# A two-layer hybrid attention trunk on one core: keys transposed and copied in four pieces, rotary roots in two, partial sums of the first squares, a new order for the first output chunk

## The chip, the cores and the metric

The kernel runs on one core of a Trainium2 chip. The metric is the device time of one execution, in microseconds (us). Three timed runs of the kernel before gave 1242.74, 1245.52 and 1246.12 us; the median is 1245.52. A core has a matrix engine (TensorE, in the profile PE, its weight loads PEld), a vector engine (VectorE, DVE), a scalar engine (ScalarE, ACT), a further vector engine (GpSimd, POOL) and an engine that here issues the transfers (SyncE, SP). Each engine runs its own instructions in the order in which the program lists them, and waits where an operand or a buffer is not ready.

## The reference

Two groups of tokens, a prompt of 512 and a sample of 256, with 1024 channels, go through two layers with the same weights. In each layer:

```
mod = silu(c) @ w_ada + b_ada ; shift, scale, gate = split(mod, 3)
hid = rms_norm(x, norm_g) * (1 + scale) + shift
qa, ka, va, za, qb, kb, vb, zb, ga, gb = split(hid @ w_in)
oa = neighbourhood attention(qa, ka, va, rpb)      # 8 heads of 64, 8 x 16 window
ya = (oa * silu(za)) @ w_pa
qh = rope(rms_norm(qb)) ; kh = rope(rms_norm(kb))  # per head, 8 query heads, 2 key heads
ob = softmax(qh kh^T / 8) vb                       # 4 query heads share a key head
yb = (ob * silu(zb)) @ w_pb
x  = x + gate * ((sigmoid(ga) * ya + sigmoid(gb) * yb) @ w_out)
```

After the second layer a last `rms_norm` gives the two outputs. All of it is float32.

## The kernel before, in words

**Precision.** TensorE gets each float32 operand as a rounded high part and a low part, and a product is three matmuls: high·high, high·low, low·high. So each weight half (128x1024) that arrives in a `raw` tile is first copied to its high part by ACT (`whi`, L222), and DVE (for a few halves POOL) subtracts to get the low part (`wlo`, L228). `split_one` issues the pair. `ahead` calls it at chosen steps of the chunk before, and `low_all` issues the waiting subtraction two steps later. Every operand that attention makes is split in the same way, with a copy on ACT and a subtraction on DVE.

**Steps.** The long stretches are built of steps (`step`): the matmuls of two 128-channel pieces of the contraction for 128 output rows, 6 matmuls of 128x512 for the prompt or 12 of 128x256 (four pieces) for the sample. After each step the program issues what is due: work put off by `defer(k, fn)` until k steps later, one piece of a `chain` (the normalisation of the next layer), attention pieces from `slots` at a set rate, and side sums of the next layer's modulation. No engine reorders anything, so the place where a piece is issued sets when it can run and what waits behind it.

**A layer.** First the values of the neighbourhood attention (`va`), then four chunks of query and key pairs with eight attention heads in slots, each head 8 slots after the one before. A head's slots 0 to 16 (`na_slots`) hold: scores, bias and row maximum, exponentials (L775) and their normalisation in slots 0 to 5; three transposes of the probabilities (`trans(0)` in slot 6, `trans(1)` in 7, `trans(2)` in 10), each copied by ACT one slot later (`ev`, L699) and completed by DVE (`el`, L704) one slot after that; the product with the values for the prompt (`pv_p`, tile `op`, slot 10) and for the sample (`pv_s`, tile `os`, slot 14). `op` and `os` share one PSUM buffer. Each is emptied by ACT (`o1`, tile `otmp`, L689) and then by DVE (`o2`, tile `oa`, L694), in slots 11 and 12 for `op` and 15 and 16 for `os`.

Then come the queries `qb` and keys and values `kvb` of the second attention with norm and rotation. `rope_part` sums squares and rotates, `rope_finish` takes the inverse square roots with three Newton rounds on DVE (L358 to L365, after L1326) and scales the rotated rows (L1333). TensorE transposes them (`qt`, `kt` by L1418) through two PSUM buffers (`ps_t`) and ACT and DVE split them into `GQ` and `GK` (L667, L668, L675, L676, L679, L680). The offsets of these pieces, in steps, stand in the table `SC`: QF, QT, QS, QST for the queries, KF for `rope_finish` of the keys, KT for their transpose, SGQ for the first slot of the grouped attention. Around them run the gate chunks `za`, whose PSUM results pass ACT (`zt`, `zh`), DVE (L1440, `zl` L1454) and POOL (L1443). The grouped attention runs in slots (`gsp` scores, maximum L902, exponential L912).

At the end of a layer the merged rows go through the output projection, four chunks for the prompt (`wo`, `feat_chunk` with `groups=(0,)`, two row blocks m of four steps each), then the sample. `merged` is split on DVE at L1563. After DP steps (last layer: DPE) the chain of the next normalisation starts: sum of squares `a_`, Newton rounds `b_` on DVE, a broadcast of the roots by matmul `c_` (tile `rb`), then one piece per channel block.

**The start.** Loads of x, of the first modulation weights (`adaraw`) and of the first weight halves are issued by SP at planned times (`load`, T0 us after the start, U us per unit). A small planner (`run_jobs`) sorts jobs of known length by earliest start, `lag` us after what they depend on. The squares of the eight 128-channel blocks of x (ACT) are added into one tile, six additions on DVE and one on POOL, and `sq_sum` sums it over partitions with four matmuls into `ssps`. WARM puts 18 matmuls of zeros (`junk`, 128x512) ahead of all, and one more every 0.45 us of planned time until 18 us.

## Time and profile before

| view | what it gives |
|---|---|
| timed runs | 1242.74, 1245.52, 1246.12 us, median 1245.52 |
| profiled execution | 1244.36 us, span from first to last instruction 1242.6 us |
| PE busy | 1208.7 us, 97% of the span, 7282 instructions |
| DVE busy | 818.4 us, 66% |
| ACT busy | 580.6 us, 47% |
| POOL busy | 347.6 us, 28% |
| mean granted TensorE clock | 0.995 |
| chain that ended last | PE 78%, DVE 11%, ACT 5% |

A row of the timeline gives start, length, engine, line, operation, output tile <- input tiles, shape and count; in brackets stands how long the engine had been idle just before, and the engine, tile and line that ended it. A row of the waits gives the engine that waited, for what, the total in us, the number of waits and the longest. A row of the windows gives the stretch, its length and, engine by engine in the order PE, PEld, DVE, ACT, POOL, the busy us with the count of instructions, then the granted TensorE clock of that stretch (PEclk, 1 is full speed), the DMA share and its GB/s.

### The profile page before, as it was taken

The page shows a single profiled execution, that of the slowest core. Times are in us where ns is not written, and L with a number is a line of the kernel's source. Part 1 is how long each engine was busy: PE and PEld are TensorE (multiplying, and loading weights), DVE is VectorE, ACT ScalarE, POOL GpSimd, SP SyncE. Part 2 cuts the span into 40 slices and gives each one's busy share as a digit, 9 for nine tenths or more (in the row PEclk, how much of TensorE's full clock was granted, in tenths as well). Part 3 has the DMA queues.
Part 4 walks back from the last instruction along what each step waited for, and adds up shares of the span by engine and source line. Part 5 has one row for each costly group of instructions (what it writes and reads, how often), then busy time and mean ns, then how long its engine had stood idle before and what let it go on. Part 6 is the DMA issues. An engine that isn't in the chain of part 4 may idle for free.

```text
span 1242.6 us, 19501 instructions
## 1 busy us (share of the span) xinstructions
PE 1208.7 (97%) x7282; PEld 1058.6 (85%) x7282; DVE 818.4 (66%) x1609; ACT 580.6 (47%) x1229; POOL 347.6 (28%) x383
## 2 busy tenths in 40 slices
PE   8999999989999999999989999998999999999997
PEld 5789988879898988887888998897988998888887
DVE  5757877775556558998384688777566545683435
ACT  4447755445545332333153776554555543232323
POOL 0024555342223121121131443553322212121102
PEclk9999999999999999999999999999999999999999
DMA  9343411111011234556352324112011113332334
GB/s 350 138 124 94 108 54 54 49 51 35 26 44 51 69 107 149 170 169 202 119 172 88 93 74 124 35 38 65 18 52 52 35 35 102 119 105 66 119 102 152
DMA packets 48125, 118.28 MB, mean 95 GB/s; under 512 B 5408, under 2 KB 11936, under 8 KB 48032
## 3 DMA queue, kind: packets, MB, share of 16 engines
q1 hardware_dynamic: 47888, 116.98, 30.6%
q8 instruction: 57, 0.93, 0.3%
q14 instruction: 36, 0.29, 0.1%
q10 hardware_dynamic: 144, 0.07, 0.0%
HBM read 110.74 MB, written 6.29 MB: 94 GB/s over the span
## 4 chain that ended last, share of the span: by engine, by line
PE 78%; DVE 11%; ACT 5%; issue 3%; DMA 1%; POOL 1%; SPq 0%; DVEq 0%; ACTq 0%; POOLq 0%
PE accp L115 35%; PE accs L115 17%; PE accw L115 8%; PE go L115 3%; PE gsp L115 3%; PE gtp L937 3%; PE acct L115 3%; DVE adaacc L445 3%; DVE wlo L228 2%; ACT p L775 1%; PE sp L115 1%; PE op L115 1%; ACT whi L222 1%; PE adap L115 1%; DVE ptl L704 1%
## 5 line engine op out<-in xcount | busy, mean ns | idle before, releaser
L115 PE MATMUL accp<-hh,whi 128*128 128x512 f32 x512 | 204.3, 399 | 0.0
L115 PE MATMUL accp<-hh,wlo 128*128 128x512 f32 x512 | 201.2, 393 | 2.1 <-DVE wlo L228 2.1
L115 PE MATMUL accp<-hl,whi 128*128 128x512 f32 x512 | 201.2, 393 | 0.0
L228 DVE TENSOR_TENSOR wlo<-raw,whi 128x1024 fp32r<-128x1024 f32 x119 | 159.1, 1338 | 21.1 <-ACT whi L222 20.5
L115 PE MATMUL accs<-hh,whi 128*128 128x256 f32 x512 | 146.4, 286 | 0.0
L115 PE MATMUL accs<-hh,wlo 128*128 128x256 f32 x512 | 145.0, 283 | 0.0
L115 PE MATMUL accs<-hl,whi 128*128 128x256 f32 x512 | 144.9, 283 | 0.0
L926 POOL TENSOR_TENSOR gp<-gp,gss 128x512 f32<-128x512 f32 x80 | 83.4, 1042 | 213.8 <-DVE gss L924 192.5
L222 ACT ACTIVATE whi<-raw 128x1024 fp32r<-128x1024 f32 x124 | 129.7, 1053 | 17.7 <-PE accw L115 8.2
L115 PEld LDWEIGHTS accp<-hh,wlo 128*128 128x128 f32 x512 | 96.8, 189 | 24.9 <-DVE wlo L228 3.8
L115 PEld LDWEIGHTS accp<-hl,whi 128*128 128x128 f32 x512 | 97.1, 190 | 17.5
L115 PEld LDWEIGHTS accp<-hh,whi 128*128 128x128 f32 x512 | 96.8, 189 | 17.7
L699 ACT ACTIVATE pth<-gtp 128x512 fp32r<-128x512 f32 x80 | 47.7, 597 | 111.2 <-PE go L115 90.2
L115 PEld LDWEIGHTS accs<-hh,whi 128*128 128x128 f32 x512 | 98.2, 192 | 1.0
L115 PEld LDWEIGHTS accs<-hl,whi 128*128 128x128 f32 x512 | 98.2, 192 | 1.0
L115 PEld LDWEIGHTS accs<-hh,wlo 128*128 128x128 f32 x512 | 98.0, 191 | 0.0
L1539 POOL TENSOR_TENSOR th<-th 128x512 f32<-128x512 f32 (+1 forms) x32 | 43.5, 1371 | 171.2 <-DVE th L1532 171.2
L445 DVE SCALAR_TENSOR_TENSOR adaacc<-adaraw,csil,adaacc 128x512 f32<-128x512 f32 x112 | 86.6, 829 | 3.6 <-DMA adaraw<-in_wsd 3.6
L722 POOL TENSOR_TENSOR bm<-u,masks 128x128 f32<-128x128 f32 (+2 forms) x80 | 41.3, 539 | 152.4 <-DMA u<-in_rpb 152.4
L704 DVE TENSOR_TENSOR ptl<-gtp,pth 128x512 fp32r<-128x512 f32 x80 | 54.7, 685 | 40.5 <-ACT pth L699 40.4
L115 PE MATMUL accw<-whi,hh 128*128 128x512 f32 x192 | 77.3, 403 | 0.0
L115 PE MATMUL accw<-wlo,hh 128*128 128x512 f32 x192 | 75.3, 392 | 0.0
(245 smaller groups left out, 2965.7 us busy)
## 6 DMA issues: line engine op xcount, KB each, us to landing
raw<-in_wst SPq DMA_DIRECT2D x124, 512.0 KB, 3.6
adaraw<-in_wsd SPq DMA_DIRECT2D x64, 256.0 KB, 3.1
adaraw<-in_wad SPq DMA_DIRECT2D x32, 256.0 KB, 6.0
u<-in_rpb SPq DMA_DIRECT2D x16, 354.5 KB, 4.8
u<-in_rpb SPq DMA_DIRECT2D x16, 236.5 KB, 4.4
out_y<-y SPq DMA_DIRECT2D x12, 256.0 KB, 2.5
x<-in_xT SPq DMA_DIRECT2D x8, 256.0 KB, 5.0
res<-in_xT SPq DMA_DIRECT2D x8, 256.0 KB, 3.0
```

The costliest lines, as they stand in the source:

```text
L115: T.matmul(out=out, lhsT=lhsT, rhs=rhs, start=start, stop=stop, skip_group_check=True)
L222: A.activation(out=hi, in_=r, func=AF.Copy)
L228: eng.tensor_sub(out=lo, in0=r, in1=hi.bitcast(F32))
L445: V.scalar_tensor_tensor(out=acc[n, h, g], in0=r, scalar=c, in1=acc[n, h, g], op0=ALU.mult, op1=ALU.add)
L699: A.activation(out=h, in_=t, func=AF.Copy)
L704: V.tensor_sub(out=lo, in0=t, in1=h.bitcast(F32))
L722: G.tensor_tensor(out=o.rearrange("p (c r) -> p c r", r=r), in0=u, in1=mk.rearrange("p (c r) -> p c r", r=r), op=ALU.add)
L775: A.activation(out=P[:, j, :], in_=P[:, j, :], func=AF.Exp, scale=-1.0, bias=ss[:, j:j + 1], accum_out=ss[:, 2 + j:3 + j])
L926: G.tensor_mul(out=pv_, in0=pv_, in1=ss[:, 4:4 + n].unsqueeze(2).to_broadcast([128, n, w]))
L937: T.transpose(t[:, q, 128 * j:128 * j + 128], src, ident)
L1539: G.tensor_add(out=t[:, sl], in0=t[:, sl], in1=mrg[k][:, sl])
```

## The change

Seven places are changed; what is computed stays the same except for the order of the sum of the first squares.

- **Start.** 16 `junk` matmuls ahead, and further ones only where the planner has a gap on PE until 20 us: 25 in place of 46. T0 goes from 3.6 to 4.3 and `lag` from 0.12 to 0.22. Of the eight squares, blocks 1 to 3 are added into 0 on DVE, 5 into 4 on POOL, and `sq_sum` runs on the four tiles 0, 4, 6 and 7.
- **Neighbourhood attention.** `pv_p`, its `o1` and its `o2` go one slot later (11, 12, 13); `trans(2)`, `ev(2)` and `el(2)` stay, and so does the sample's part.
- **Rotary part.** `newton` can be called in parts. `rope_finish` does the first half of the roots at once, the second half one step later, and the scaling of the i-th tile 2 + i steps later. QF 5 to 4, QT 9 to 10, QS 6 to 5, QST 12 to 11.
- **Keys.** KF 7 to 5, KT 13 to 9, SGQ 16 to 13. The transpose of the prompt's keys is issued at KT, that of the sample's two steps later, and in each the copy of the second key head follows one step after the first.
- **Weights.** For chunks whose contraction has four pieces (`pa`, `pb`), `ahead` is called after steps 2 and 4, not 3 and 6.
- **First output chunk.** `late=True`: the last step of both row blocks comes after all others.
- **Next layer's norm.** An empty piece between `b_` and `c_`, and DP 6 to 5: in the first layer's prompt `a_` and `b_` come one step earlier and `c_` where it was; for the sample and at the end of the last layer, `c_` comes one step later.

```diff
 SC = dict(
-    T0=3.6,
+    T0=4.3,
-    WARM=(18, 18.0, 0.45),
+    WARM=(16, 20.0),
-    QF=5,
-    QT=9,
+    QF=4,
+    QT=10,
-    QS=6,
-    QST=12,
-    KF=7,
-    KT=13,
-    SGQ=16,
+    QS=5,
+    QST=11,
+    KF=5,
+    KT=9,
+    SGQ=13,
-    DP=6,
+    DP=5,
...
     def paired(pieces):
-        return pieces[0:3] + [sum(pieces[i:i + 2], []) for i in range(3, len(pieces), 2)]
+        return pieces[0:4] + [sum(pieces[i:i + 2], []) for i in range(4, len(pieces), 2)]
...
-        return [[a_], [b_], [c_]]
+        return [[a_], [b_], [], [c_]]
...
+            kk = per * (1 + g)
+            seq = [(m, k0) for m in range(2) for k0 in range(0, nk, kk)]
+            if late:
+                seq = [p for p in seq if p[1] < nk - kk] + [p for p in seq if p[1] == nk - kk]
+            for m, k0 in seq:
...
-                        if not (keep and name[2] == 3) and cnt[0] in ((3, 6) if len(groups) == 2 else (3, 5) if groups[0] == 0 else (2, 3)):
+                        if not (keep and name[2] == 3) and cnt[0] in ((2, 4) if nk == 4 else (3, 6) if len(groups) == 2 else (3, 5) if groups[0] == 0 else (2, 3)):
                             ahead(name)
...
-        at(10, pv_p)
         at(10, lambda: trans(2))
-        at(11, lambda: o1(NP))
+        at(11, pv_p)
         at(11, lambda: ev(2))
-        at(12, lambda: o2(0, NP))
+        at(12, lambda: o1(NP))
         at(12, lambda: el(2))
+        at(13, lambda: o2(0, NP))
         at(14, pv_s)
...
-        def run_jobs(lag=0.12):
+        def run_jobs(lag=0.22):
...
+            n0, until = SC["WARM"]
+            t = 2.0 + 0.35 * n0
+            for j in sorted((j for j in jobs if j["eng"] == "PE"), key=lambda j: done[j["n"]]):
+                start = done[j["n"]] - j["dur"]
+                while t + 0.5 < min(start, until):
+                    out.append((t, -1, lambda: warm(1)))
+                    t += 0.3
+                t = max(t, done[j["n"]])
+            warm(n0)
...
-        jg = job("POOL", 1.2, [js[2], js[3]], lambda: sq_add(0, 3, 2, G), 1)
-        j = js[0]
-        for k, d in ((1, js[1]), (4, js[4]), (2, jg), (5, js[5]), (6, js[6]), (7, js[7])):
-            j = job("DVE", 0.75, [j, d], lambda k=k: sq_add(0, k, 0, V), 1)
-        j = job("PE", 0.95, [j], sq_sum, 0)
+        ja = js[0]
+        for k in range(1, 4):
+            ja = job("DVE", 0.85, [ja, js[k]], lambda k=k: sq_add(0, k, 0, V), 1)
+        jb = job("POOL", 1.3, [js[4], js[5]], lambda: sq_add(0, 5, 4, G), 1)
+        jsum = []
+        for k, d in ((0, ja), (4, jb), (6, js[6]), (7, js[7])):
+            jsum.append(job("PE", 0.95, [d] + jsum[-1:], lambda k=k: sq_sum(k, k == 0, k == 7), 0))
...
             def rope_finish(rs, ss):
...
-                y = newton(ss.rearrange("p t h -> p (t h)"), n * nh).rearrange("p (t h) -> p t h", h=nh)
+                y, parts = newton_parts(ss.rearrange("p t h -> p (t h)"), n * nh)
...
+                roots()
+                defer(1, roots2)
...
+                    defer(2 + i, lambda r=r, k=k, t=t: V.tensor_mul(
+                        out=r, in0=r, in1=yv[:, t:t + k, :].unsqueeze(3).to_broadcast([128, k, nh, 64])))
...
+            def ktr(g):
+                c, n = RNG[g]
...
+                evac_k(GK[0][0], GK[0][1], 0, t, slice(c, c + n))
+                defer(1, lambda: evac_k(GK[1][0], GK[1][1], 1, t, slice(c, c + n)))
...
             defer(SC["KF"], kfin)
-            defer(SC["KT"], ktr)
+            defer(SC["KT"], lambda: ktr(0))
+            defer(SC["KT"] + 2, lambda: ktr(1))
...
                 feat_chunk(("wo", l, i), merged, KC, lambda m, g, ps, i=i: wev(m, g, ps, i), groups=(0,),
-                           keep=i >= 2)
+                           keep=i >= 2, late=i == 0)
```

**PE at the start.** `adap` are the first modulation products (four matmuls of one pair of loads), `adat` their columns, `ssps` the sum of squares, `rb` the broadcast of its roots. Before:

```order
L115 MATMUL junk<-cst 128x512 x29
L115 MATMUL adap<-adaraw,c_104 32x256 x4
L115 MATMUL junk<-cst 128x512 x3
L115 MATMUL adap<-adaraw,c_104 32x256 x4
L115 MATMUL junk<-cst 128x512 x2
L115 MATMUL ssps<-ones,sq 128x1 x4
L115 MATMUL junk<-cst 128x512 x2
L115 MATMUL adat<-sel,rows 128x2 x2
L115 MATMUL junk<-cst 128x512
L115 MATMUL adap<-adaraw,c_104 32x256 x4
L115 MATMUL junk<-cst 128x512
```

After the change:

```order
L115 MATMUL junk<-cst 128x512 x22
L115 MATMUL ssps<-ones,sq 128x1 x8
L115 MATMUL adap<-adaraw,c_104 32x256 x4
L115 MATMUL ssps<-ones,sq 128x1 x4
L115 MATMUL adap<-adaraw,c_104 32x256 x8
L115 MATMUL ssps<-ones,sq 128x1 x4
L115 MATMUL adat<-sel,rows 128x2 x2
L115 MATMUL adap<-adaraw,c_104 32x256 x4
L115 MATMUL junk<-cst 128x512 x3
L115 MATMUL adap<-adaraw,c_104 32x256 x4
L115 MATMUL rb<-ident,ny 128x128 x4
```

The one group of four `ssps` becomes four groups, two of them ahead of the first product, one behind it and one behind the third. The junk between the products is gone but for three, and `rb`, which came after four products, comes after five.

**ACT around the end of the second neighbourhood head**, first layer. `p,ss` are exponentials of the next head, `pth` the high part of a transpose, `Q` query copies of a chunk. Before:

```order
L667 ACTIVATE Q<-accp 64x128
L667 ACTIVATE Q<-accp 64x384
L689 ACTIVATE otmp<-op 64x512
L699 ACTIVATE pth<-tp 128x512
L775 ACTIVATE p,ss<-p,ss 128x256 x2
L222 ACTIVATE whi<-raw 128x1024
L667 ACTIVATE Q<-accp 64x128
L667 ACTIVATE Q<-accp 64x384
L775 ACTIVATE p,ss<-p,ss 128x256 x2
L689 ACTIVATE otmp<-os 64x256
```

After the change:

```order
L680 ACTIVATE Q<-accp 64x128
L680 ACTIVATE Q<-accp 64x384
L712 ACTIVATE pth<-tp 128x512
L788 ACTIVATE p,ss<-p,ss 128x256 x2
L222 ACTIVATE whi<-raw 128x1024
L680 ACTIVATE Q<-accp 64x128
L680 ACTIVATE Q<-accp 64x384
L702 ACTIVATE otmp<-op 64x512
L788 ACTIVATE p,ss<-p,ss 128x256 x2
L702 ACTIVATE otmp<-os 64x256
```

The copy of `op` (`otmp<-op`, 64x512) moved behind a transpose, two exponentials, a weight half and two query copies; the copy of `os`, which needs the same PSUM buffer, stays where it was and has two instructions between.

**The key stage on PE**, first layer. `accs` and `accp` are the sample's and the prompt's rows of the gate chunk, `kt` the transposes of the keys. Before:

```order
L115 MATMUL accs<-hh_699,whi 128x256
L115 MATMUL accs<-hl_700,whi 128x256
L115 MATMUL accs<-hh_699,wlo 128x256
L115 MATMUL accp<-hh_343,whi 128x512
L115 MATMUL accp<-hl_344,whi 128x512
L115 MATMUL accp<-hh_343,wlo 128x512
L115 MATMUL accp<-hh_356,whi 128x512
L115 MATMUL accp<-hl_357,whi 128x512
L115 MATMUL accp<-hh_356,wlo 128x512
L1418 MATMUL kt<-ident,rr 128x128 x6
L115 MATMUL accp<-hh_415,whi 128x512
```

After the change:

```order
L115 MATMUL accs<-hh_655,whi 128x256
L115 MATMUL accs<-hl_656,whi 128x256
L115 MATMUL accs<-hh_655,wlo 128x256
L1446 MATMUL kt<-ident,rr 128x128 x4
L115 MATMUL accs<-hh_674,whi 128x256
L115 MATMUL accs<-hl_675,whi 128x256
L115 MATMUL accs<-hh_674,wlo 128x256
```

The key transposes stood behind the 48 `accs` of the first gate chunk and the first 6 `accp` of the next one; now the prompt's four stand behind 12 of these `accs`, three sample steps and one prompt step earlier, and the sample's two come two steps after them.

**DVE in the same stage.** `rr` are the scaled keys that `kt` reads, `zl` and `zt` the gate chunk, `GK` the low parts of the keys. Before:

```order
L1333 TENSOR_TENSOR rr<-rr,ny 128x512
L1333 TENSOR_TENSOR rr<-rr,ny 128x256
L1454 TENSOR_TENSOR zl<-zt,zh 128x512
L1440 SCALAR_TENSOR_TENSOR zt<-zt,accp 128x512
L1454 TENSOR_TENSOR zl<-zt,zh 128x512
L679 TENSOR_TENSOR GK<-kt,GK 64x512
L680 TENSOR_TENSOR GK<-kt,GK 64x512
L679 TENSOR_TENSOR GK<-kt,GK 64x512
L680 TENSOR_TENSOR GK<-kt,GK 64x512
L679 TENSOR_TENSOR GK<-kt,GK 64x256
```

After the change:

```order
L1470 SCALAR_TENSOR_TENSOR zt<-zt,accp 128x512
L228 TENSOR_TENSOR wlo<-raw,whi 128x1024
L1365 TENSOR_TENSOR rr<-rr,ny 128x512
L1365 TENSOR_TENSOR rr<-rr,ny 128x256
L1484 TENSOR_TENSOR zl<-zt,zh 128x512
L692 TENSOR_TENSOR GK<-kt,GK 64x512
L693 TENSOR_TENSOR GK<-kt,GK 64x512
L1470 SCALAR_TENSOR_TENSOR zt<-zt,accp 128x512
L692 TENSOR_TENSOR GK<-kt,GK 64x512
L693 TENSOR_TENSOR GK<-kt,GK 64x512
L692 TENSOR_TENSOR GK<-kt,GK 64x256
L693 TENSOR_TENSOR GK<-kt,GK 64x256
```

The low parts of the second key head follow a gate piece, and ahead of the scaling of the keys stand a gate piece and a weight half that stood ahead of the roots before.

More of the change, by code (lines that the diff above doesn't have):

```diff
@@ L365, in newton @@
             V.scalar_tensor_tensor(out=y, in0=a, scalar=1.5, in1=y, op0=ALU.add, op1=ALU.mult)
+        return y, [first, refine, refine, refine]
+    def newton(x, n):
+        y, parts = newton_parts(x, n)
+        for fn in parts:
+            fn()
         return y
@@ L563, in wide_pass, with feat_chunk @@
         wts.pop(name)
-    def feat_chunk(name, src, nk, evac, ksteps=2, groups=(0, 1), keep=False, sep=False):
+    def feat_chunk(name, src, nk, evac, ksteps=2, groups=(0, 1), keep=False, sep=False, late=False):
         cur = {}
@@ L583, in feat_chunk @@
         for g in groups:
-            for m in range(2):
-                kk = per * (1 + g)
-                for k0 in range(0, nk, kk):
+            kk = per * (1 + g)
[3 more added lines that the diff above has]
+            for m, k0 in seq:
                     def f(g=g, m=m, k0=k0, kk=kk):
@@ L1149, in sq_add, with sq_sum @@
             gfree(sq.pop((g, k)))
-        def sq_sum():
-            hcell["ps"] = ps_acc.tile([128, 4], F32, tag="acc", name="ssps")
+        def sq_sum(k, first, last):
+            if first:
+                hcell["ps"] = ps_acc.tile([128, 4], F32, tag="acc", name="ssps")
             for i in range(4):
-                mm(hcell["ps"][:, i:i + 1], sq[0, 0][:, 128 * i:128 * i + 128], ones[:, 0:1], i == 0, i == 3)
-            gfree(sq.pop((0, 0)))
+                mm(hcell["ps"][:, i:i + 1], sq[0, k][:, 128 * i:128 * i + 128], ones[:, 0:1],
+                   first and i == 0, last and i == 3)
+            gfree(sq.pop((0, k)))
         js = [job("ACT", 0.63, [], lambda k=k: square(0, k), 1, tx[k]) for k in range(KC)]
-        jg = job("POOL", 1.2, [js[2], js[3]], lambda: sq_add(0, 3, 2, G), 1)
-        j = js[0]
-        for k, d in ((1, js[1]), (4, js[4]), (2, jg), (5, js[5]), (6, js[6]), (7, js[7])):
-            j = job("DVE", 0.75, [j, d], lambda k=k: sq_add(0, k, 0, V), 1)
-        j = job("PE", 0.95, [j], sq_sum, 0)
-        jsum = [j]
-        for (fn,), (eng, dur) in zip(rms_chain(0, hcell)[1:], (("DVE", 2.4), ("PE", 1.0))):
+        ja = js[0]
[5 more added lines that the diff above has]
+            jsum.append(job("PE", 0.95, [d] + jsum[-1:], lambda k=k: sq_sum(k, k == 0, k == 7), 0))
+        j = jsum[-1]
+        for (fn,), (eng, dur) in zip([p for p in rms_chain(0, hcell)[1:] if p], (("DVE", 2.4), ("PE", 1.0))):
             j = job(eng, dur, [j], fn, 0)
@@ L1195, in sample_sum @@
             sums[0][0]()
-        sums = rms_chain(1, scell)
+        sums = [p for p in rms_chain(1, scell) if p]
         j = job("PE", 0.4, jadd + [jfin[0, 3], jfin[1, 3], jva[-6]], sample_sum, 0)
```

53 lines of the change are left out of this document (23 added, 30 removed).

## The prediction

> **What bounds the kernel now.** First the page's busy time, then the waits of PE.
>
> ```profile
> span 1242.6 us, 19501 instructions
> PE 1208.7 (97%) x7282; PEld 1058.6 (85%) x7282; DVE 818.4 (66%) x1609; ACT 580.6 (47%) x1229; POOL 347.6 (28%) x383
> ```
>
> ```profile
> PE gsp L115 <- ACT gp L912: 5.6, 2, 3.6
> PE op L115 <- DVE ptl L704: 5.2, 4, 1.6
> PE gsp L115 <- DVE GK L680: 4.1, 2, 2.0
> PE rb L115 <- DVE ny L365: 3.1, 2, 1.7
> PE accp L115 <- DVE wlo L228: 2.7, 5, 1.0
> PE adap L115 <- DMA adaraw<-in_wad: 1.4, 1, 1.4
> ```
>
> PE is the bound: 97% busy, and its matmuls stay the same but for some junk. So the change can only win PE's stops. These six rows hold 22.1 us, and each has an edit that touches it. A stop costs some 0.15 us beyond its idle time, since the matmul that restarts lasts longer (0.39 against 0.28 in the first row below). The second thing to win is the clock, which falls behind two of the stops:
>
> ```profile
> 165.80 0.39 PE L115 MATMUL op<-ptl,v 128*128 128x256 f32 x1 [1.00 <-DVE ptl L704]
> 201.12 0.39 PE L115 MATMUL op<-ptl,v 128*128 128x256 f32 x1 [1.61 <-DVE ptl L704]
> 247.94 0.50 PE L115 MATMUL gsp<-GK,GQ 128*128 128x512 f32 x1 [2.03 <-DVE GK L680]
> 256.60 0.80 PE L115 MATMUL gsp<-GK,GQ 128*128 128x512 f32 x2 [3.60 <-ACT gp L912]
> 854.25 0.64 PE L115 MATMUL gsp<-GK,GQ 128*128 128x512 f32 x1 [2.03 <-DVE GK L680]
> 862.92 0.73 PE L115 MATMUL gsp<-GK,GQ 128*128 128x512 f32 x2 [2.04 <-ACT gp L912]
> ```
>
> ```profile
> 248.00:250.00 2.00, 2.00 (x9) 1.66 (x10) 1.96 (x4) 0.00 (x0) 0.00 (x0) 1.00 0.00 0
> 258.00:260.00 2.00, 2.00 (x7) 1.55 (x6) 1.16 (x5) 1.22 (x3) 1.20 (x2) 0.50 0.44 74
> 856.00:858.00 2.00, 2.00 (x7) 1.58 (x5) 1.93 (x6) 0.00 (x0) 0.10 (x1) 0.53 0.00 0
> ```
>
> In these windows (the eighth figure is the granted clock) seven matmuls start in 2 us at half clock, nine at full clock: behind 256.60 and 854.25 six or seven 128x512 matmuls stand 0.43 us apart in place of 0.23, with the slower ones around them about 1.7 us in each layer. The 2.03 us stop at 247.94 left the clock at 1.00, the equal one at 854.25 did not.
>
> **Keys and rotary part.** The four rows from 201.12 on show what goes: in the first layer 1.76 + 2.18 + 3.75 + 1.7 (clock) = 9.4, in the second the same 1.76 (its stop is one of the four in the second row of the waits), 2.18 + 2.19 + 1.7, so 7.8; together 17.2. What comes in their place? Each edit asks DVE for the keys earlier:
>
> ```profile
> 212.00:240.00 28.00, 28.00 (x191) 25.84 (x190) 24.92 (x57) 13.04 (x28) 11.39 (x14) 1.00 0.21 64
> 233.59 0.28 PE L115 MATMUL accs<-hh,whi 128*128 128x256 f32 x1
> 240.74 0.82 PE L1418 MATMUL kt<-ident,rr 128*128 128x128 f32 x6
> 223.86 1.39 DVE L668 SCALAR_TENSOR_TENSOR GQ<-qt,GQ 64x512 fp32r<-64x512 f32 x2
> 234.44 1.26 DVE L1326 TENSOR_SCALAR qss<-qss 128x12 f32<-128x12 f32 x1
> 233.47 2.21 POOL L1443 TENSOR_TENSOR zt<-zt,oa 128x512 f32<-128x512 f32 x1 [0.18 <-DVE zt L1440]
> 238.08 1.03 DVE L1333 TENSOR_TENSOR rr<-rr,ny 128x512 f32<-128x512 f32 x2
> ```
>
> The first `kt` moves from 240.74 to 12 `accs` matmuls (0.12 each, 1.44) after 233.59: PE wants it at 235.0. It reads `rr`, and DVE's list ahead of `rr` is as long as before: it runs at 238.08, or 1.1 earlier if the small L1326 doesn't again last 1.26 while POOL works on the gate (the second part, 0.17, follows that end). With half of the 1.03 for the first tile, `rr` is there at 237.5, so PE stops 2.5 us. The bounds: nothing, if DVE uses up its 28 − 24.92 = 3.1 idle us in this stretch; 2.5 + 1.8 = 4.3, if PE brings along the 1.76 won at 201.12 and DVE doesn't. I take 2.8, as DVE is 89% busy. The queries add a second stop: two steps fewer lie between the prompt's last `qt` and the sample's first, and that needs a PSUM buffer which DVE empties with L668 late in this same list; between 0 and one such pair and its copy, 2.8; I take 1.2. With 0.15 this makes 4.1 a layer, 8.2 in both, and I count one clock drop (1.7) for two stops of 2.8, which lie between the 2.03 that dropped it once of two times and the 3.60 that did. Behind `kt`, the scores come 5.7 us later (three steps of 1.44 and one of 1.37), while the copies of one head need 2 x 0.59 and 2 x 0.69, so the old stop at 247.94 doesn't return; the one at 256.60 was DVE and ACT being late from the eight copies in a row, and these are now spread. Sum: 17.2 − 8.2 − 1.7 = **+7.3**.
>
> On the clock the Trainium skill says something else ("TensorE: Matmul & The Clock Gate", section on what is actually happening): the gate closes after an idle window of about 3.4 us, so a 2.8 us stop would cost no clock and the sum would be 9.0. The trace disagrees in one row, where 2.03 us were enough; I keep the 1.7.
>
> **Neighbourhood heads.** `pv_p` one slot later gives `ptl` a step (1.4 us) more: the stop at 165.80 and its like in the second layer go, 2 x 1.15 = +2.3. But `op` and `os` share a PSUM buffer, and `os` stays:
>
> ```profile
> 114.34 0.59 ACT L689 ACTIVATE otmp<-op 64x512 f32<-64x512 f32 x1
> 116.44 1.05 ACT L222 ACTIVATE whi<-raw 128x1024 fp32r<-128x1024 f32 x1
> 117.51 0.65 ACT L667 ACTIVATE Q<-accp 64x128 fp32r<-64x128 f32 x2
> 115.97 0.69 DVE L694 SCALAR_TENSOR_TENSOR oa<-op,otmp 64x512 f32<-64x512 f32 x1
> 118.20 0.28 PE L115 MATMUL os<-pth,v 128*128 128x256 f32 x1
> ```
>
> In the second head the copy of `op` now stands behind the second pair of Q. Without it that pair ends 0.6 earlier, at 117.55; the copy ends at 118.15 and `oa` (0.69) near 118.9, while PE wants `os` at 118.20: a new wait of 0.75. It holds the whole PE queue, since all later steps stand behind. Over two layers −1.5; the bounds are 0 (the rest of ACT's list has room) and −2.5 (the next heads, with less than 1 us left, wait too). Net **+0.8**.
>
> **Weights, the output chunk and the next norm.**
>
> ```profile
> 482.02 0.50 PE L115 MATMUL accp<-hh,wlo 128*128 128x512 f32 x1 [0.25 <-DVE wlo L228]
> 1087.58 0.50 PE L115 MATMUL accp<-hh,wlo 128*128 128x512 f32 x1 [1.04 <-DVE wlo L228]
> 568.84 0.50 PE L115 MATMUL accp<-ml,whi 128*128 128x512 f32 x1 [1.32 <-DVE ml L1563]
> 623.90 1.16 PE L115 MATMUL rb<-ident,ny 128*128 128x128 f32 x8 [1.42 <-DVE ny L365]
> 648.33 0.71 PE L115 MATMUL rb<-ident,ny 128*128 128x128 f32 x4 [1.69 <-DVE ny L365]
> 619.75 1.63 DVE L358 TENSOR_SCALAR ny<-ms 128x4 int32<-128x4 int32 x1
> 618.86 2.49 POOL L228 TENSOR_TENSOR wlo<-raw,whi 128x1024 fp32r<-128x1024 f32 x1 [1.09 <-ACT whi L222]
> ```
>
> The five `wlo` stops, 2.7 us and 5 x 0.15 (two of them are shown), are each shorter than the step or two by which `ahead` moves, so all go: **+3.4**; if ACT's or DVE's queue is the late one they stay (0). The last step of the first output block behind seven others gives `ml` far more than 1.32: **+1.5**. The first `rb` keeps its step while its roots start one step of 1.4 us earlier, but L358 (1.63 in place of 0.17) ends only with POOL's `wlo`, whose place doesn't move: of 1.57 I count +0.5 (0 to 1.57). The second gets a step of its own, +1.5 of 1.84. Together **+2.0**.
>
> **The start.**
>
> ```profile
> 11.04 1.22 PE L115 MATMUL adap<-adaraw,c 128*32 128x256 f32 x8 [1.43 <-DMA adaraw<-in_wad]
> 10.00:12.00 2.00, 0.96 (x8) 0.32 (x8) 1.69 (x4) 0.83 (x2) 0.00 (x0) 1.00 1.05 396
> 24.84 0.50 PE L115 MATMUL accw<-whi,hh 128*128 128x512 f32 x1
> 24.00:40.00 16.00, 16.00 (x133) 10.65 (x126) 10.37 (x21) 7.70 (x16) 0.00 (x0) 1.00 1.04 392
> ```
>
> From 24 to 40 us PE and the transfers (share 1.04) are both full, so only what happens ahead of 24.84 can win, and the loads pace that: junk taken away mostly leaves PE waiting for the same loads. The first roots still wait for the last square. The bounds are −2 (the last partial sum stands behind a product that waits for its load, by as much as the 1.43 of the stop at 11.04 and a product) and +2 (1.43 and one product won); I take **+0.6**, a single product of about 0.6 (half of the 1.22 for a pair).
>
> **Sum.** 7.3 + 0.8 + 3.4 + 1.5 + 2.0 + 0.6 = 15.6. The profiled execution took 1244.36, so 1228.8; the runs' median of 1245.52 is 1.2 above it, so about 1229.5 as a median.
>
> **Rivals.**
> - *Clean key stage.* DVE uses its 3.1 idle us and neither `kt` nor `qt` stops, so the 8.2 and the clock's 1.7 come on top: 1219.5. For it speaks that ACT is busy for only 13.04 of the 28 us; against it DVE's 24.92.
> - *DVE holds the key stage.* `kt` 4.3, `qt` 2.8 and a clock drop in both layers: 17.2 − 2 x (7.4 + 1.7) = −1.0 in place of 7.3, total 7.3: 1238.
> - *Nothing.* The same, and the `rb` and start terms at their lower ends: 7.3 − 2.0 − 2.6 = 2.7: 1243.
> - *Slower: the clock at the start.* 21 of the 46 junk matmuls are gone, and between 7 and 24 us PE has only short groups between waits. If the clock stays at half, the 16.0 us of PE work in the window from 24 to 40 last twice as long, +16, and the products and `rb` before them add about 4: +20 − 15.6 = 4.4, about 1250. It decides if the granted clock is still near 0.5 at 24.84. For it: 2.03 us of idleness halved it at 854.25. Against it: the 1.43 stop at 11.04 left it at 1.00, the 16 + 6 junk ahead remain, and 1.7 us of dense work opened it again each time. The Trainium skill's page named above, section on HAM oscillation, warns of gaps over 3.4 us; with that few such gaps fit here.
>
> **How the numbers follow.** Main forecast 0.53, clean stage 0.18, DVE-held stage 0.17, nothing 0.07, slower 0.05. Main's own range goes from 1224 (`kt` and `qt` at half, +4.1, no `os` wait, +1.5) to 1234 (a second clock drop, −1.7, `os` at its bound, −1.0, `rb` at nothing, −2.0). For 8 in 10 I go to 1219 and 1239. About 0.3% (3.7 us) is what a measurement can tell from no change: the first three cases are beyond it, so faster 0.88, same 0.07, slower 0.05.
>
> **What would show it.** Right: no `gsp` row with an idle time over 1 us in the key stage, a `kt` row with 2 to 4 us behind `rr`, an `os` row in the second head with some 0.75 behind `oa`, no `wlo` or `ml` rows among PE's waits. Wrong: a `kt` row without wait, the old `gsp` stops still there, a window before 40 us with a clock under 0.9, or new stops at scores because the softmax is behind.

## The result

The changed kernel takes 1256.62 us (median of 4 runs, 1253.5 to 1257.46) against 1245.33 for the kernel before (4 runs): a ratio of 1.009, 95% interval 1.0067 to 1.0112. It is slower by 11 us, where 16 us of gain were forecast. PE is busy for 1213.7 us, 5.0 more than before, and the span grew by 12.2 us to 1254.8.

The waits of PE in the changed kernel (what waited, for what; total us, times, longest):

```profile
PE sp L115 <- DVE ss L781: 7.5, 6, 1.7
PE kt L1446 <- DVE rr L1365: 5.8, 2, 2.9
PE os L115 <- DVE oa L707: 3.8, 4, 1.6
PE qt L1406 <- DVE GQ L681: 3.3, 2, 1.7
PE ssps L115 <- POOL sq L1171: 2.3, 1, 2.3
PE rb L115 <- DVE ny L369: 1.9, 2, 1.6
PE accs L115 <- POOL wlo L228: 1.8, 2, 1.6
PE gsp L115 <- ACT gp L925: 1.6, 2, 1.3
```

Nearly every row at which the edits aimed is gone or shorter: no `op`, no `accp <- wlo`, no `ml`, no `gsp <- GK`; `rb` keeps one stop of 1.64 us. In their place stand others. The timeline of PE shows them in order, from the start to the end of the first layer:

```profile
12.40 1.05 PE L115 MATMUL ssps<-ones,sq 128*128 128x1 f32 x8 [2.27 <-POOL sq L1171]
118.68 0.36 PE L115 MATMUL sp<-Kh,Q 128*128 128x256 f32 x1 [1.66 <-DVE ss L781]
126.05 0.39 PE L115 MATMUL os<-pth,v 128*128 128x256 f32 x1 [1.59 <-DVE oa L707]
176.78 0.38 PE L115 MATMUL sp<-Kh,Q 128*128 128x256 f32 x1 [1.59 <-DVE ss L781]
232.99 0.30 PE L1406 MATMUL qt<-ident,rr 128*128 128x128 f32 x1 [1.67 <-DVE GQ L681]
249.92 1.09 PE L1446 MATMUL kt<-ident,rr 128*128 128x128 f32 x4 [2.90 <-DVE rr L1365]
638.16 0.39 PE L115 MATMUL accs<-mh,wlo 128*128 128x256 f32 x1 [1.60 <-POOL wlo L228]
656.00 0.71 PE L115 MATMUL rb<-ident,ny 128*128 128x128 f32 x4 [1.64 <-DVE ny L369]
```

Behind the first of these stops the granted clock (the eighth figure) is at half for ten us:

```profile
14.00:24.00 10.00, 10.00 (x60) 6.34 (x57) 3.34 (x15) 1.82 (x3) 0.00 (x0) 0.51 1.02 369
```

Where the time went is seen when the same matmul is looked up in both timelines (start in us):

| matmul | before | changed | later by | so the stage ahead of it |
|---|---|---|---|---|
| first `accw` | 24.84 | 28.89 | 4.05 | start +4.1 |
| first `accw` of the queries | 154.69 | 164.16 | 9.47 | heads, first layer, +5.4 |
| a gate chunk behind the grouped attention | 420.09 | 429.75 | 9.66 | queries and keys +0.2 |
| an `accp` of the last `pa`/`pb` chunks | 552.17 | 559.92 | 7.75 | weights −1.9 |
| first pair chunk, second layer | 672.03 | 678.32 | 6.29 | output, norm −1.5 |
| its `accw` of the queries | 760.84 | 772.68 | 11.84 | heads +5.6 |
| behind its grouped attention | 1024.85 | 1037.84 | 12.99 | queries and keys +1.2 |
| last output chunk | 1206.66 | 1218.67 | 12.01 | weights −1.0 |

The last heads still run beside the queries. Counted to the last `os` of each layer (209.22 and 815.53 before, 217.92 and 826.43 changed) the heads cost 4.7 and 4.6 us, and the queries and keys behind them 1.0 and 2.1.

### The profile page after: what moved, and what is told of

Its sections match the earlier page's. It is cut to its first block, busy times and chain, and to the rows that moved or that the text cites. A ratio compares the mean times of both kernels' runs of the same rounds, so it can differ in the third digit from the quotient of the medians.

```text
span 1254.8 us, 19456 instructions
## 1 busy us (share of the span) xinstructions
PE 1213.7 (97%) x7285; PEld 1060.8 (85%) x7285; DVE 814.5 (65%) x1606; ACT 580.0 (46%) x1229; POOL 348.8 (28%) x383
## 3 DMA queue, kind: packets, MB, share of 16 engines
HBM read 110.74 MB, written 6.29 MB: 93 GB/s over the span
## 4 chain that ended last, share of the span: by engine, by line
PE 79%; DVE 10%; ACT 5%; issue 2%; DMA 2%; POOL 1%; SPq 0%; DVEq 0%; ACTq 0%; POOLq 0%
PE accp L115 36%; PE accs L115 17%; PE accw L115 9%; PE go L115 3%; PE gsp L115 3%; PE gtp L950 3%; PE acct L115 2%; DVE wlo L228 2%; ACT p L788 1%; PE sp L115 1%; DMA raw<-in_wst 1%; DVE GQ L681 1%; PE adat L115 1%; PE op L115 1%; DVE ptl L717 1%
```

## The experiments

In each, the kernel before ran on the same chip, and ratios are against it.

**The parts alone.** Four kernels, each the one before with one part of the diff.

```diff
-    T0=3.6,
+    T0=4.3,
-    WARM=(18, 18.0, 0.45),
+    WARM=(16, 20.0),
...
+            jsum.append(job("PE", 0.95, [d] + jsum[-1:], lambda k=k: sq_sum(k, k == 0, k == 7), 0))
```

> The kernel before with the start part alone (16 junk matmuls ahead and gaps only, planner's lag and T0, the four partial sums). Theory: with the junk gone PE stops about 2 us for POOL's sum of the squares, the clock halves from about 14 to 24 us, and the first accw comes about 4 us later than the 24.84 of before: +4 us in all. Rival: the 2.27 us stop was the chance of late loads in one execution, and the start is worth what was predicted, -0.6 us (between -2 and +1). A granted clock near 0.5 between 14 and 24 us speaks for the theory, 1.00 for the rival.

1247.38 against 1243.53 us, ratio 1.0029 (1.0014 to 1.0044): +3.9 us, spread from 1243.3 to 1250.9. The profiled execution was the fastest, had no such wait and a clock of 1.00; the mean clock of the seven others lay at 0.989 to 0.991, where it is 0.995 before. So the start costs in most executions and not by one late load, and their lower mean clock points to the clock; no profile of this kernel shows such an execution.

```diff
-        at(10, pv_p)
         at(10, lambda: trans(2))
-        at(11, lambda: o1(NP))
+        at(11, pv_p)
         at(11, lambda: ev(2))
-        at(12, lambda: o2(0, NP))
+        at(12, lambda: o1(NP))
         at(12, lambda: el(2))
+        at(13, lambda: o2(0, NP))
```

> The kernel before with the neighbourhood part alone (product with the values, its copy and its sum one slot later). Theory: the new stops at sp and os that the changed kernel shows come from this part, +4 to +5 us a layer, +8 to +10 us in all, with the two stops at op (1.0 us) gone. Rival, as predicted: the op stops go (-2.3), os waits 0.75 us a layer, -0.8 us in all; the sp stops then come from another part. The rows of sp with an idle time decide.

1259.45 us, ratio 1.0130 (1.0117 to 1.0143): +16 us, more than the whole change. The six `sp` stops (7.5 us) and the `os` stops are all here, so they come from this part. ACT's timeline of this kernel points to a cause:

```profile
100.31 0.50 ACT L786 ACTIVATE p<-p,ss 128x256 f32<-128x256 f32 x1
103.01 0.60 ACT L710 ACTIVATE pth<-tp 128x512 fp32r<-128x512 f32 x1 [2.11 <-PE op L115]
104.61 0.60 ACT L700 ACTIVATE otmp<-op 64x512 f32<-64x512 f32 x1
```

The copy `pth` of the third transposes waits 2.11 us for PE's `op`, from which it reads nothing. `pth` comes from a pool of two buffers (`ptp`), and both hold the transposes that `op` is still to read. Before, `op` was issued a slot ahead of this copy; now it is issued in the same slot, so ACT stands until PE has come to `op` and finished it, and everything behind it in ACT's and then DVE's queue is late.

```diff
-    QST=12,
-    KF=7,
-    KT=13,
-    SGQ=16,
+    QST=11,
+    KF=5,
+    KT=9,
+    SGQ=13,
...
+                defer(1, roots2)
...
-            defer(SC["KT"], ktr)
+            defer(SC["KT"], lambda: ktr(0))
+            defer(SC["KT"] + 2, lambda: ktr(1))
```

> The kernel before with the rotary and key part alone (roots in two, keys in four pieces, new offsets). Prediction on record: -7.3 us, kt waits about 2.8 us a layer and the old stops at gsp go. Reading of the changed kernel: qt waits 2 us, kt 2.9 us, a clock drop in one layer, and the scores afterwards return less than was thought: between 0 and +4 us in all.

1242.93 us, ratio 0.9994 (0.9986 to 1.0003): no difference that can be told. The old stops at `op` (1.61 us) and for `GK` are gone, the one for `gp` is down to 1.31 us in each layer, and these rows stand in the first layer (the second is alike):

```profile
223.31 0.30 PE L1396 MATMUL qt<-ident,rr 128*128 128x128 f32 x1 [1.69 <-DVE GQ L679]
223.94 0.85 PE L1396 MATMUL qt<-ident,rr 128*128 128x128 f32 x3 [0.34 <-DVE rr L1355]
240.47 0.63 PE L1436 MATMUL kt<-ident,rr 128*128 128x128 f32 x4 [1.57 <-DVE rr L1355]
253.30 0.73 PE L115 MATMUL gsp<-GK,GQ 128*128 128x512 f32 x2 [1.31 <-ACT gp L923]
```

The clock behind the first two, in the window from 224 to 227 us of this kernel (the eighth figure):

```profile
224.00:227.00 3.00, 3.00 (x9) 2.51 (x10) 2.49 (x5) 2.51 (x8) 0.00 (x0) 0.51 0.02 5
```

```diff
-        return [[a_], [b_], [c_]]
+        return [[a_], [b_], [], [c_]]
...
-    DP=6,
+    DP=5,
...
-                        if not (keep and name[2] == 3) and cnt[0] in ((3, 6) if len(groups) == 2 else (3, 5) if groups[0] == 0 else (2, 3)):
+                        if not (keep and name[2] == 3) and cnt[0] in ((2, 4) if nk == 4 else (3, 6) if len(groups) == 2 else (3, 5) if groups[0] == 0 else (2, 3)):
...
-                           keep=i >= 2)
+                           keep=i >= 2, late=i == 0)
```

> The kernel before with the three small parts together (ahead after steps 2 and 4, the first output chunk's last steps late, the next norm's empty piece and DP 5). Prediction on record: -6.9 us (3.4 + 1.5 + 2.0). Reading of the changed kernel: the wlo stops of pa and pb go (-3), ml goes (-1.5), but the second rb still waits 1.6 us and a new wait of 1.6 us for POOL's wlo stands ahead of it: -4 to -5 us.

1239.2 us, ratio 0.9967 (0.9955 to 0.9979): −4.3 us, as expected, though not by the stops that were expected: no `rb` stop is left between the layers, and PE waits 1.94 us for POOL's `wlo`, with a clock drop behind it. The four parts alone sum to +3.9 + 15.9 − 0.6 − 4.3 = +14.9, against +11.3 for the whole. The heads-only profile has one stop that the whole hasn't, a second `rb` of 3.32 us with a clock drop behind it:

```profile
654.65 1.22 PE L115 MATMUL rb<-ident,ny 128*128 128x128 f32 x4 [3.32 <-DVE ny L369]
```

By its timeline the heads (up to the last `os`) cost 6.2 us in the first layer and 6.1 in the second, and the stretch from the first `rb` to the first score of the second layer another 4.5.

**Why the heads cost.**

```diff
-        at(11, lambda: ev(2))
         at(12, lambda: o1(NP))
-        at(12, lambda: el(2))
+        at(12, lambda: ev(2))
         at(13, lambda: o2(0, NP))
+        at(13, lambda: el(2))
```

> The neighbourhood part alone, but the copy of the third transposes (ev, pth) and its low part (el) also one slot later, so that every piece keeps its order behind the product with the values. In the heads-only run ACT's copy pth waited 2.11 us for PE's op: the pool of pth has two buffers, and the third transposes need the one that op still reads. Theory (ACT held by that buffer, and everything behind it late): the 2.1 us wait of ACT and the six stops at sp (7.5 us) go, os waits less than the 1.59 us in the second head; within -2 to +3 us of the kernel before. Rival (the eight op matmuls, 0.95 us, are missing on PE ahead of the third scores, and DVE is late by itself): the sp stops stay above 1 us each, +10 to +16 us like the heads-only run.

1251.59 us, ratio 1.0059 (1.0045 to 1.0072): half of the loss is gone, from +16 to +7.5 us. ACT now waits for `op` with the copy that needs it, and the next `pth` follows at once. ACT's timeline:

```profile
103.06 0.59 ACT L700 ACTIVATE otmp<-op 64x512 f32<-64x512 f32 x1 [1.43 <-PE op L115]
103.67 0.60 ACT L710 ACTIVATE pth<-tp 128x512 fp32r<-128x512 f32 x1
```

The `os` stops of 1.59 and 0.33 us went (one of 0.27 for `ptl` is left in each layer). The `sp` stops did not all go, as PE's timeline of the first layer shows:

```profile
113.73 0.36 PE L115 MATMUL sp<-Kh,Q 128*128 128x256 f32 x1 [0.98 <-DVE ss L779]
168.43 0.39 PE L115 MATMUL sp<-Kh,Q 128*128 128x256 f32 x1 [1.59 <-DVE ss L779]
```

So both ideas held in part. About 8 us go with the copy moved along. By the timelines of the two profiled executions the heads now cost 2.0 and 1.8 us in place of 6.2 and 6.1, and the stretch behind the first `rb` 2.2 in place of 4.5. What is left in the heads stands where `op`'s eight matmuls (0.95 us) stood between two scores: the third score needs a buffer that DVE empties, and now comes to it about a microsecond sooner. The second row looks like the old stop of 1.00 us at `op` in a new place: PE no longer waits there for DVE's `ptl`, but 1.59 us for DVE's maximum behind it.

```diff
-        at(11, lambda: o1(NP))
         at(11, lambda: ev(2))
-        at(12, lambda: o2(0, NP))
+        at(12, lambda: o1(NP))
         at(12, lambda: el(2))
+        at(13, lambda: o2(0, NP))
```

> The kernel before with only the copy and the sum of op (o1, o2) one slot later; the product itself, the transposes and their copies stay. It gives the price of the late copy alone. By the prediction's working os waits 0.75 us a layer in the second head: +1.5 us in all, no stop at sp, the op stops of 1.0 and 1.6 us stay. If the os stop is 1.6 us here too, the late copy alone makes it and not the wait of ACT.

`os` stops 0.52 us in each layer (0.75 was expected) and no `sp` does. A `wlo` stop of 0.40 comes with it. The time is 1249.91 us, ratio 1.0045 (1.0030 to 1.0059), +5.9 us, more than these stops. By the timeline the heads cost 1.5 and 1.4 us, the second layer's stop for `gp` 1.5 (3.59 us in place of 2.04), and the stretch behind the first `rb` 2.1: there the second `rb` waits 2.19 us in place of 1.69, with a clock drop, as it does in all three heads kernels (2.19 to 3.32). POOL's `wlo` (2.40 us) runs 0.7 us later against the first `rb` than before, and beside it one of DVE's small operations that lead to the roots takes 2.35 us, where the others take 0.17; why `wlo` runs later was not settled.

**Why the start costs.**

```diff
     WARM=(18, 18.0, 0.45),
-    T0=3.6,
+    T0=4.3,
...
+        for k, d in ((0, ja), (4, jb), (6, js[6]), (7, js[7])):
```

> The start part with the junk matmuls of before (18 ahead and one each 0.45 us until 18 us), but the partial sums, T0 and lag of the change. The start-only run spread from 1243.3 to 1250.9 us with the mean clock at 0.995 in its fastest and 0.989 to 0.991 in most others. Theory (without junk a wait for loads or for a sum of squares closes the clock gate in some executions): the spread falls to that of the kernel before (1242.6 to 1247.6), median within 1.5 us of it. Rival (the order of the partial sums itself delays the roots): the median stays 3 to 4 us above.

1246.93 us, ratio 1.0027 (1.0013 to 1.0041), spread from 1244.96 to 1254.82: the old junk doesn't mend it. Seven of the twelve executions had a mean clock of 0.994 or 0.995, as before the change, and still took 1246.35 us in the median, 2.3 above the kernel before; so the sums cost about 2 us beside the clock, by their length or their order. Only two of the twelve had a mean clock of 0.986 to 0.987 (the others 0.992 to 0.995), where with the new junk seven of eight were at 0.991 or less. The profiled one is one of the two:

```profile
12.00:28.00 16.00, 16.00 (x68) 9.31 (x68) 3.34 (x15) 1.71 (x3) 0.00 (x0) 0.50 1.05 385
```

PE shows busy for 16.00 of 16 us, at half clock throughout.

```diff
-    T0=3.6,
+    T0=4.3,
-    WARM=(18, 18.0, 0.45),
+    WARM=(16, 20.0),
...
-        def run_jobs(lag=0.12):
+        def run_jobs(lag=0.22):
```

> Of the start part only the junk, T0 and lag; the squares are summed on DVE as before. The start with partial sums cost 3.9 us with the new junk and 2.9 us with the old junk. Theory now (the partial sums cost by themselves: 32 matmuls of one column in place of 8 on PE and a sum on POOL that PE waits for; the junk sets how often the clock drops on top): within 2 us of the kernel before, with some executions at a mean clock near 0.99. Rival (missing junk is the cause and the partial sums are harmless): +3 us or more, like the start-only run.

1244.20 against 1244.18 us, ratio 1.0000 (0.9992 to 1.0009), ten of eleven executions at 0.995 and one at 0.992. So the missing junk alone costs nothing. The partial sums are the cause, and beside them the junk seems to decide how often the clock falls (two of twelve executions against seven of eight). In the same stretch as above:

```profile
12.00:28.00 16.00, 15.38 (x119) 8.58 (x118) 11.01 (x29) 6.10 (x10) 0.00 (x0) 1.00 1.05 391
```

The partial sums do two things: they add twelve one-column matmuls (24 instructions in the trace, two for each), and they put PE's queue behind squares and POOL. The next kernel does only the first.

```diff
                 mm(hcell["ps"][:, i:i + 1], sq[0, 0][:, 128 * i:128 * i + 128], ones[:, 0:1], i == 0, i == 3)
+            for _ in range(3):
+                for i in range(4):
+                    mm(junk[:, i:i + 1], sq[0, 0][:, 128 * i:128 * i + 128], ones[:, 0:1], True, True)
```

> The kernel before with 12 more one-column sums (the same squares against the ones, written into the junk tile) behind the four of the first sum. The start part brought 12 such sums, and with them a clock near 0.5 from 12 or 14 us on in some executions, with the new junk and with the old; less junk alone left the clock at 1.00 and the time unchanged. Theory (one-column matmuls count as next to no work for the clock gate): mean clock under 0.992 in some executions, the median 2 to 6 us above. Rival (the sums' order and PE's wait for POOL cost, the matmuls are harmless): only their own length, about 12 x 0.23 = 3 us at most on a stretch that the loads pace, clock 0.995 throughout, 0 to +2 us.

1250.19 us, ratio 1.0046 (1.0031 to 1.0060): +5.9 us, and every execution at a mean clock of 0.991 to 0.993. PE's timeline and the windows behind it:

```profile
14.98 3.55 PE L115 MATMUL junk<-ones,sq 128*128 128x1 f32 x24
```

```profile
14.00:16.00 2.00, 2.00 (x20) 1.96 (x18) 0.71 (x5) 0.14 (x1) 0.00 (x0) 1.00 1.05 404
16.00:18.00 2.00, 2.00 (x16) 2.00 (x15) 1.25 (x8) 0.00 (x0) 0.00 (x0) 0.72 1.04 386
18.00:20.00 2.00, 2.00 (x9) 1.81 (x9) 0.00 (x0) 0.00 (x0) 0.00 (x0) 0.50 1.08 392
```

No stop stands in the three microseconds ahead of the drop. The clock falls while PE shows busy with one-column matmuls, so by this trace they do not hold it up. In the kernel before, the four sums take 0.81 us (14.22 to 15.03), so twelve more would take an estimated 2.4 us at full clock; `rb` comes 5.67 us later (24.62 against 18.95), which leaves about 3.2 us for the clock. In the start part itself the two things are not separated. Its profiled execution ran the same sums with no stop at a clock of 1.00, the changed kernel lost the clock behind the stop of 2.27 us, and the run with the old junk lost it with no stop over 0.2 us between PE's first matmul and the drop.

**What the key stage can give.** The diff is against the changed kernel.

```diff
-    T0=4.3,
+    T0=3.6,
-    WARM=(16, 20.0),
+    WARM=(18, 18.0, 0.45),
...
+        at(10, pv_p)
         at(10, lambda: trans(2))
-        at(11, pv_p)
```

> The change without the start part and without the neighbourhood part. If the parts add up: -0.6 (keys) and -4.3 (weights, chunk, norm) = -5 us, near 1238.6. The new waits at qt and kt (1.6 to 2.0 us each) with a clock drop in each layer stay.

Ratio 0.9954 (0.9941 to 0.9967), 1238.6 us: what is left of the change wins 5.4 us, as the parts said. The next five build on it: the first diff is against this kernel, and the others follow from the kernel that their expectation names.

```diff
-    QST=11,
+    QST=13,
     KF=5,
-    KT=9,
-    SGQ=13,
+    KT=11,
+    SGQ=15,
```

> The change without its start and neighbourhood parts, and with three offsets put later: QST 11 to 13, KT 9 to 11, SGQ 13 to 15. Against the run without start and heads (1238.6 us). Theory (the edits ask DVE for queries and keys two steps too early, and each stop there is followed by a clock drop in some layers): the stops at qt (2.0 us) and kt (2.9 us) go in both layers, with one clock drop; 8 to 12 us less, 1227 to 1231 us. Rival (DVE bounds the whole key stage, so the wait only moves to the scores): gsp waits 2 us or more in each layer again and the time stays within 3 us of 1238.6.

1230.70 us, ratio 0.9894 (0.9879 to 0.9909): 13.5 us faster than the kernel before, the best of the study. The `qt` stop is gone. The `kt` stop is not: 2.96 us in each layer, both with a clock drop, though the transposes are issued two steps later: PE no longer loses 2.0 us at `qt`, so it comes to `kt` only about 0.5 us later than in the kernel without start and heads, and `rr` comes as much later. There is no `gsp` stop at all.

```diff
-    QF=4,
-    QT=10,
+    QF=5,
+    QT=9,
...
-    QS=5,
-    QST=13,
+    QS=6,
+    QST=12,
```

> The same, but all four query offsets as in the kernel before (QF 5, QT 9, QS 6, QST 12), KF 5, KT 11, SGQ 15. The query stops of the change: if they come from the two steps that QT 10 and QST 11 took from between the prompt's last and the sample's first transposes, QST 12 behind QT 9 has the old distance and shows no stop at qt, but the prompt's op stop of 1.6 us (the roots of the queries one step later) may come back: within 3 us of the run with all three later.

Here the first query transposes stand ahead of the scaling of two of the four prompt tiles, so these go in unscaled; the amount of work is the same. 1235.18 us, ratio 0.9929 (0.9917 to 0.9942), 4.5 us more than with the later offsets. The old distance does not help: `qt` now waits 2.98 us for `rr` of the sample, whose roots (QS 6) come a step later. The prompt's `op` stop did not come back, but `qt` waits there, 0.83 and 0.42.

```diff
-        return [[a_], [b_], [], [c_]]
+        return [[a_], [b_], [c_]]
...
-    DP=5,
+    DP=6,
```

> The kernel with the three later offsets, but without the edit on the next layer's norm (the empty piece and DP). It prices that edit: the prediction had it at +2.0 us of gain, so this kernel would be 2 us slower than the one with it. Reading of the traces so far: it takes 1.2 and 1.2 to 1.7 us from the two rb stops and pays 1.5 to 1.9 us for POOL's wlo, sometimes with a clock drop: between 1.5 us slower and 1 us faster.

1231.75 us, ratio 0.9898 (0.9885 to 0.9912), against 0.9894 with the edit on the norm: it is worth about 1 us, less than these intervals can tell from nothing. PE's `rb` rows without the edit, and then PE's rows of the same place with it (the kernel with three later offsets):

```profile
615.17 1.16 PE L115 MATMUL rb<-ident,ny 128*128 128x128 f32 x8 [1.42 <-DVE ny L369]
639.56 0.71 PE L115 MATMUL rb<-ident,ny 128*128 128x128 f32 x4 [1.65 <-DVE ny L369]
```

```profile
613.38 1.16 PE L115 MATMUL rb<-ident,ny 128*128 128x128 f32 x8 [0.24 <-DVE ny L369]
623.57 0.39 PE L115 MATMUL accs<-mh,wlo 128*128 128x256 f32 x1 [1.61 <-POOL wlo L228]
640.20 0.71 PE L115 MATMUL rb<-ident,ny 128*128 128x128 f32 x4 [0.36 <-DVE ny L369]
```

It takes 2.5 us from the two `rb` stops and pays 1.6 at POOL's `wlo`, which PE now reaches sooner.

```diff
-    KT=11,
-    SGQ=15,
+    KT=13,
+    SGQ=17,
```

> As the kernel with the three later offsets (1230.7 us), but KT 13 and SGQ 17. There kt still stopped 2.96 us for rr in both layers, each followed by a clock drop; the transposes stand now two steps of 1.4 us later. Theory (DVE brings rr at a fixed time, PE only asks too early): the kt stop shrinks to 0.2 us or less and the clock stays at 1.00, 2 x (2.9 + 1.3) = 8 us less, near 1223 us. Rival (DVE falls behind by as much again, since its own list waits on PE): a stop of 1 us or more stays at kt or moves to gsp, less than 4 us won.

1237.57 us, ratio 0.9944 (0.9931 to 0.9958): 7 us slower than with KT 11, where 8 less were expected. The `kt` stop shrank to 0.17, as the theory had it, but the wait only moved on, as the rival had it:

```profile
239.78 0.63 PE L1438 MATMUL kt<-ident,rr 128*128 128x128 f32 x4 [0.17 <-DVE rr L1357]
254.83 1.22 PE L115 MATMUL gsp<-GK,GQ 128*128 128x512 f32 x2 [3.73 <-ACT gp L925]
419.04 0.39 PE L115 MATMUL go<-pth,vg 128*128 128x256 f32 x1 [1.28 <-DVE ob L707]
```

The clock adds to it. Behind the 3.73 us it stands at 0.53, 0.50, 0.50 and 0.76 in the four windows of 2 us from 254 on; with KT 11, behind `kt`, it stood at 0.78, 0.50 and 0.86 in three.

```diff
-    SGQ=17,
+    SGQ=16,
```

> The same with SGQ 16, the value of the kernel before: the scores come three steps behind kt in place of four. It tells whether the split copies let the scores follow at the distance at which the kernel before stopped 2.0 us at gsp. Theory: the four-piece copies are done in time, no gsp stop over 0.5 us, within 1.5 us of the one with SGQ 17. Rival: gsp waits about 1 to 2 us for GK in each layer, 2 to 4 us slower than it.

1233.89 us, ratio 0.9915 (0.9901 to 0.9930), and not slower but 3.7 us faster than with SGQ 17. The first score waits 0.35 for `GK`, so the copies in four pieces do let it follow at three steps (2.03 before). The second waits 3.46 us for `gp`, nearly the 3.60 of the kernel before. ACT brings `gp` when DVE has the maximum `gss`, and DVE has it behind the gate chunk and the low parts of the keys. What holds these up differs from before, as the rows of DVE and ACT show. Before:

```profile
241.38 0.59 ACT L675 ACTIVATE GK<-kt 64x512 fp32r<-64x512 f32 x1 [4.54 <-PE kt L1418]
245.26 0.62 ACT L1450 ACTIVATE zh<-zt 128x512 fp32r<-128x512 f32 x1
245.91 0.69 DVE L1454 TENSOR_TENSOR zl<-zt,zh 128x512 fp32r<-128x512 f32 x1 [5.60 <-ACT zh L1450]
253.34 0.68 DVE L902 TENSOR_REDUCE gss<-gsp 128x1 f32<-128x512 f32 x1
```

With KT 13 and SGQ 16:

```profile
244.83 0.59 ACT L688 ACTIVATE GK<-kt 64x512 fp32r<-64x512 f32 x1 [1.56 <-DVE GK L693]
246.07 0.70 DVE L692 TENSOR_TENSOR GK<-kt,GK 64x512 fp32r<-64x512 f32 x1 [0.55 <-ACT GK L689]
249.64 0.38 ACT L688 ACTIVATE GK<-kt 64x256 fp32r<-64x256 f32 x1 [1.87 <-DVE GK L693]
250.44 0.43 DVE L692 TENSOR_TENSOR GK<-kt,GK 64x256 fp32r<-64x256 f32 x1 [0.84 <-ACT GK L689]
251.34 0.69 DVE L915 TENSOR_REDUCE gss<-gsp 128x1 f32<-128x512 f32 x1
```

Before, ACT made the eight copies without a break, and DVE stood idle for 5.60 us until `zh` came behind them. Spread out, the copies wait on each other: ACT's copies of the second key head for DVE's low parts of the first, and DVE's next low parts for these copies. Why ACT's copies need those low parts, which read the same `kt`, no run shows. The key part alone shows the same, with 1.57 and 1.53 us on ACT and 0.55 and 0.84 on DVE. So ahead of `kt` DVE is full (busy for 11.45 of the 12 us from 228 to 240 with KT 13 and SGQ 16), but between `kt` and the maximum it is not. By the stops at `kt` and at the first scores the stage still owes 2.96 us a layer with KT 11, 3.9 with KT 13 and SGQ 17, and 4.0 with SGQ 16. Of the offsets tried, none removes it.

## Why the prediction was wrong

**The heads** were the largest miss: +0.8 forecast, −16 measured alone (12.3 of it in the heads by the timeline, 4.5 behind the first `rb`) and −9.3 by the timeline of the changed kernel. The step that failed is "a new wait of 0.75. It holds the whole PE queue", with bounds of 0 and −2.5. The `os` wait was there and of that size (0.52 alone); the bounds left out two other waits. `pth` has two buffers, and moving `op` behind the third transposes made their copy wait for `op` (2.11 us on ACT; about 8 of the 16 us went in the run that moved the copy along). And `op`'s 0.95 us had been cover for DVE ahead of the third score, as far as the stops of 0.98 and 1.59 us that are still there in that run tell. The change's order showed `pth<-tp` ahead of `otmp<-op` on ACT; what was not asked is which buffer it writes. That "the stop at 165.80 and its like in the second layer go" was right by its row and wrong as a gain: the wait for DVE came back at `sp` a few microseconds on.

**The keys**: +7.3 forecast, 0.6 measured alone. Of the "17.2" the stops at `op` and for `GK` go, but 1.31 us a layer stay of the stop for `gp`, which the sum put at nothing. "I take 2.8" for `kt` was close in the changed kernel (2.90, 2.91) and too much in the part alone (1.57, 1.69). The term that was mis-sized is `qt`, 1.2 forecast, 1.69 + 0.34 measured, with a clock drop behind it in both layers of the part alone, where one drop was counted for both layers. Together the stops come to 4.9 us a layer in place of 4.0. The step that failed is "these are now spread". The old stop at 256.60 was indeed made by the eight copies in a row: DVE stood 5.60 us behind them. But spread, the copies wait on each other, and the stop is 1.31 us in the part alone and back at 3.5 to 3.7 when `kt` doesn't take the wait. "DVE holds the key stage" was the rival that came nearest here by its sum (17.2 taken, 18.2 given back); it was given 0.17. Its stops of 4.3 and 2.8 were not reached (at most 2.98 and 2.03 with the change's offsets or later ones), and behind `kt` DVE was not full.

**The start**: +0.6 forecast, −3.9 measured. The rival of the clock at the start named the right effect, half clock from 14 to 24 us, with a smaller price than its 20 us, since the clock was back (0.90 in the window from 24 to 26 us) ahead of the long matmuls, which start at 28.89. It named the wrong cause, "21 of the 46 junk matmuls are gone": less junk alone costs nothing. The step that failed is the price of the partial sums: "the last partial sum stands behind a product" counts only their place in the queue. The part with the sums costs 3.9 us and the one without them nothing, and one-column sums can take the clock away by themselves. Whether they or the stop of 2.27 us did it in the changed kernel stays open; the stop is not needed for it, since the kernels with the sums and the old junk, and with more sums alone, lost the clock with no stop over 0.4 us between PE's first matmul and the drop. Against this rival the prediction set that "1.7 us of dense work opened it again each time". That 1.7 is the time lost: by the windows of 2 us from 256 on (0.78, 0.50, 0.87) the clock stayed at half for about 3.4 us.

**Weights** and **output chunk**: right. All five `accp` stops for `wlo` and the `ml` stop are gone; 3.8 us and 1.7 us by the timelines with and without (3.4 and 1.5 forecast).

**The norm**: +2.0 forecast, about 1 measured, within the noise. The step that failed is a wait that the sum left out. "+1.5 of 1.84" for the second `rb` and the first one's gain were right in the profile with later offsets (1.29 and 1.18 us). Left out was POOL's `wlo`, 1.6 us, a few microseconds behind the first `rb` and until then hidden by its stop.

The sum gives 1245.52 − 15.6 = 1229.9 as a median, not 1229.5; nothing hangs on that.

On the clock, the rule of the Trainium skill's page "TensorE: Matmul & The Clock Gate" (section on what is actually happening) would have put the keys at 9.0, further off still. It has the gate close after an idle window of about 3.4 us, while here `qt` stops of 1.69 and 0.34 us were followed by half clock. The page also says that the window runs freely. That the same stop can fall differently fits this: 2.90 us at `kt` was followed by half clock in the first layer of the changed kernel, 2.91 in the second was not.

## What to carry to other kernels

When a step is moved behind another, list for each instruction it passes the buffers that both touch, in SBUF pools as well as PSUM, and not only the operands; then ask which wait was hidden by the time the moved step took where it stood. A stop of an engine that waits for a nearly full one is not removed by asking elsewhere for the same result: take the sum of its waits in the stage, and search the offsets for the place where the remaining one costs least. Copies in a row on one engine are not made cheaper by spreading them between another engine's work if each then waits for the other's; look up what each copy waits for. An edit is to be timed alone before it is joined to others: two of the four parts here lost 20 us between them and hid that the rest, with three offsets moved, wins 13.5.
